# A two-layer diffusion trunk on eight cores: whole-tensor stages replaced by block streams that a list scheduler interleaves, with host-side layouts

## The chip, the cores and the metric

The kernel runs on all 8 cores of one Trainium2 chip; each core takes two of the 16 prompts and one of the 8 samples, and all share the weights. There is no traffic between cores. The metric is the time of the slowest core in device microseconds (us), as the median of several runs.

Runs come in two states. In the slow one the cores of a die show a lower granted TensorE clock (recorded in the trace as a share of full speed) and the time is longer: in the changed kernel's one slow run die 0 had 0.915 to 0.938 and die 1 0.945 to 0.964, and it took 1306.38 us where the median is 1277.59.

## The reference, cut to what matters

```
# 1536 tokens a core: two context sequences of 256, one latent sequence of 1024; D_MODEL = 1024
for i in range(DEPTH):                        # DEPTH = 2
    shift/scale/gate = ada_terms(cond, ada_w[i], ada_b[i])      # silu(cond) @ (1024 x 6144): "ada" below
    h = rms_norm(x, norm_mix_g[i]) * (1 + scale) + shift
    if i % 2 == 0:                            # pooling mixer beside latent attention
        u, cq, ckv, krope = ab_split(h, w_in)          # 512 + 384 + 256 + 32 columns
        y_pool = multi_scale_pool(u, pool_w, pool_scale)         # windows 2, 4, 8, 16
        q = rms_norm((rms_norm(cq) @ w_uq) per head)             # 8 heads of 64 + 32 rotary
        k = rms_norm(concat(ckv @ w_ukv, krope) per head); v = ckv @ w_ukv
        y = concat(y_pool, softmax(q k^T / sqrt(96)) v) @ w_out  # latent: 512 cached + 1024 own keys
    else:                                     # gated MLP over chunks of 128 tokens
        u, v = split(h @ gm_w_in); y = (u * (w_s rms_norm(v) + b_s)) @ gm_w_out
    x = x + gate * y
    x = x + gate2 * swiglu(rms_norm(x) modulated, wg, wu, wd)    # FFN, 2816 wide
```

The outputs are x for context and latent tokens, and the normalised `ckv` and the `krope` of the context.

## The kernel before

Every stage works on the whole tensor of 1536 tokens, and a stage begins when the one before it is through. x arrives token-major and is transposed on TensorE; its twelve tiles pass through a ring of four staging buffers.

```python
def load_transposed(src, ntile, F, dst3, ...):
    for i in range(ntile):
        P.dma("sp", st[:], src[i * 128:(i + 1) * 128, :], ...)
        ...
        P.tr(ps[...], st[:, fc * 128:fc * 128 + fp], ident[:])      # f32 transpose on TensorE
        P.cp(evac_engs[k % 2], dst3(f0, nb, i, fp), ps[...])

def xnorm(es2, l, w, hT, small=False):       # all three blocks, then the next stage
    for b in range(3):
        for kc in range(8):
            ... square on ScalarE or VectorE; P.mm(ps[:], ones[:], sq[:], ...)
        rstd(rs[:], ps[:], 1024)
        for kc in range(8): ... multiply, scale, shift
# ... [cut]
# attention: each head alone is projected, squared, normalised and rotated (72 such units)
def projq(ps, h=h, ...):
    P.mmg(ps[0:96, 0:n], [(wuq[:, kc, h * 96:(h + 1) * 96], cqn[:, kc, ...]) for kc in range(3)])
# ... [cut]
for hl in range(4):
    for (q0, n) in qblocks:
        for kt in range(nkt + 1):
            if kt < nkt:
                P.mm(S[:, 0:n], kT[0:96, hl, ...], qT[0:96, hl, q0:q0 + n])
                P.act(pt[:, 0:n], S[:, 0:n], AF.Exp, scale=float(96.0 ** -0.5))
            if pend is not None:
                P.mm(O[:, 0:n], Vsb[:, pk, hl, :], ppt[:, 0:n], ...)
        P.recip(rd[64:128, 0:n], O[64:128, 0:n])                     # softmax denominator, VectorE
        P.tt("dve", yab[0:64, ...], O[0:64, 0:n], rd[64:128, 0:n], ALU.mult)
        ada_piece(pool=(5, 6, 7))                                    # ring of three weight slots
```

Two helper lines recur in the profile: nearly all matmuls are recorded at L210, all ScalarE activations at L227.

## Time and profile before

| | before |
|---|---|
| fast runs | 1732 to 1744 us, median near 1740 |
| slow runs | one at 1793 us, the others 1866 to 1905 us |
| profiled run (fast, slowest core) | 1742.7 us |
| first input projection | 122 us |
| exps of attention, first to last | 346 to 710 us |
| first FFN matmul | 779 us |
| last matmul of the second FFN | 1702 us |

The prediction shows the busy shares and the stages. Three more lines carry the table: the answer for the exp tiles (count, duration in ns as least, median and most, first and last start), the row of the windows for the end (length, then busy us of PE, PEld, DVE, ACT, POOL, granted clock, DMA share, GB/s), and the count of DMA packets.

```profile
L227 ACT ACTIVATE pt<-pb x224: 378/597/597, 346.1 to 709.6; 128x512 bf16<-128x512 f32 x96, 128x256 bf16<-128x256 f32 x16
```
```profile
1702.00:1742.70 40.70, 14.72 (x98) 13.57 (x96) 8.98 (x14) 6.54 (x12) 0.00 (x0) 0.71 0.38 155
```
```profile
DMA packets 117684, 92.17 MB, mean 53 GB/s; under 512 B 4512, under 2 KB 104480, under 8 KB 117600
```

The exps are spread over 364 us, though 224 of at most 0.6 us need no more than 134. The last 41 us are output transposes and stores. Most packets are under 2 KB (104480 of 117684), because weight pieces are cut out of row-major matrices.

### The profile page before, as it was taken

The numbers are of one execution on the slowest core, as the hardware profiler recorded it, in microseconds if no ns is written. First come the engines' busy times: TensorE is split into PE (matmuls) and PEld (weight loads), VectorE is DVE, ScalarE is ACT, GpSimd is POOL, SyncE is SP. The second block draws the span as 40 slices with busy tenths as digits, with TensorE's granted clock in tenths as the row PEclk, the third lists the DMA queues.
The fourth block names the chain that finished last, engine by engine and source line by source line (L and its number), as shares of the span: only waits on it lengthen the run. The fifth ranks groups of instructions, "written<-read, shape, count | busy, mean of one in ns | idle before, by whom it ended". The sixth has DMA issues, their size and how long they took to land.

```text
span 1742.7 us, 17547 instructions; the slowest of 8 cores (1714.4 to 1742.7 us)
## 1 busy us (share of the span) xinstructions
PE 1320.0 (76%) x6107; PEld 573.0 (33%) x6211; DVE 677.6 (39%) x965; ACT 482.8 (28%) x884; POOL 320.9 (18%) x288
## 2 busy tenths in 40 slices
PE   3335661366877876959999999878847899999994
PEld 2202320133222221324444444323312344444443
DVE  1261224155444544462223243741825421424262
ACT  1141221244656656242110100143502311010101
POOL 1021106311620540032100000040421410000000
PEclk9757885555678669979999999979968899999997
DMA  9608642574040052007632313003060553340103
GB/s 193 121 0 97 87 52 73 81 97 61 1 61 13 0 90 32 0 0 104 89 49 40 46 25 49 1 6 49 1 97 0 85 82 52 54 55 2 24 1 145
DMA packets 117684, 92.17 MB, mean 53 GB/s; under 512 B 4512, under 2 KB 104480, under 8 KB 117600
## 3 DMA queue, kind: packets, MB, share of 16 engines
q0 software_dynamic: 110304, 72.10, 30.8%
q1 hardware_dynamic: 7296, 18.94, 3.2%
q8 instruction: 54, 0.88, 0.2%
q14 instruction: 30, 0.25, 0.1%
HBM read 156.24 MB, written 6.88 MB: 94 GB/s over the span
## 4 chain that ended last, share of the span: by engine, by line
PE 63%; DMA 11%; ACT 9%; DVE 8%; issue 5%; POOL 3%; ACTq 0%; SPq 0%; DVEq 0%; POOLq 0%
PE pb L210 60%; DMA adaw<-ada_w 5%; ACT pt L227 3%; PE pb L208 2%; ACT rsh L227 2%; DMA y<-ostg 2%; POOL hT L241 2%; DVE xtmp L231 1%; POOL S L231 1%; DMA ldt<-cckv 1%; DMA gwo<-gm_w_out 1%; ACT xrs L227 1%; DVE gtb L231 1%; ACT hT L227 1%; DMA ldt<-x_in 1%
## 5 line engine op out<-in xcount | busy, mean ns | idle before, releaser
L210 PE MATMUL pb<-hT,wgs 128*128 128x512 bf16 x1042 | 249.6, 380 | 1.0 <-POOL hT L241 0.2
L210 PE MATMUL pb<-hT,wus 128*128 128x512 bf16 x1029 | 247.1, 379 | 1.4
L248 DVE SCALAR_TENSOR_TENSOR xT<-pb,mod,xT 128x512 f32<-128x512 f32 x240 | 179.9, 751 | 149.0 <-PE pb L210 143.9
L210 PE MATMUL pb<-apart,wdb 128*128 128x512 bf16 x1035 | 227.6, 379 | 1.1
L231 DVE TENSOR_TENSOR apart<-pb,sg 128x512 bf16<-128x512 f32 x132 | 91.1, 691 | 352.8 <-PE pb L210 349.3
L227 ACT ACTIVATE sg<-pb 128x512 f32<-128x512 f32 x132 | 78.4, 597 | 484.3 <-PE pb L210 484.3
L210 PEld LDWEIGHTS pb<-hT,wgs 128*128 128x128 bf16 x1056 | 103.6, 98 | 126.4 <-issue 3.2
L210 PEld LDWEIGHTS pb<-apart,wdb 128*128 128x128 bf16 x1056 | 103.3, 98 | 124.6
L210 PEld LDWEIGHTS pb<-hT,wus 128*128 128x128 bf16 x1056 | 103.3, 98 | 124.4
L227 ACT ACTIVATE pt<-pb 128x512 bf16<-128x512 f32 (+1 forms) x224 | 117.9, 565 | 86.3 <-PE pb L210 84.6
L241 POOL TENSOR_SCALAR hT<-xtmp,AA,mod 128x512 bf16<-128x512 f32 x48 | 72.3, 1514 | 344.3 <-ACT hT L227 179.2
L260 DVE RECIPROCAL rd<-pb 64x256 f32<-64x256 f32 (+1 forms) x32 | 81.7, 2552 | 102.2 <-PE pb L210 102.1
L210 PE MATMUL pb<-pt,Vsb 128*128 128x512 bf16 (+1 forms) x214 | 84.9, 407 | 42.3 <-ACT pt L227 39.7
L210 PE MATMUL pb<-xsq,ones 128*128 128x512 bf16 x92 | 41.4, 545 | 84.1 <-ACT xsq L227 68.7
L210 PE MATMUL pb<-qT,kT 96*128 96x512 bf16 (+1 forms) x224 | 87.2, 414 | 10.4 <-DVE Vsb L254 4.7
L200 POOL DMA_DIRECT2D adaw<-ada_w x48 | 42.3, 883 | 237.9 <-PE pb L210 200.6
L231 DVE TENSOR_TENSOR xtmp<-xT,xrs 128x512 f32<-128x512 f32 x96 | 65.2, 727 | 37.8 <-ACT xrs L227 26.1
L227 ACT ACTIVATE xsq<-xT 128x512 bf16<-128x512 f32 x48 | 29.3, 624 | 179.5 <-PE pb L210 147.8
L210 PE MATMUL pb<-scT,adaw 128*128 128x2 bf16 x768 | 27.3, 165 | 57.5 <-DMA adaw<-ada_w 57.0
L210 PE MATMUL pb<-hT,w_in 128*128 128x512 bf16 (+1 forms) x230 | 68.9, 448 | 1.2 <-issue 0.8
L200 POOL DMA_DIRECT2D wgs<-ffn_wg x22 | 19.5, 888 | 262.8 <-PE pb L210 262.8
L210 PEld LDWEIGHTS pb<-pt,Vsb 128*128 128x128 bf16 x224 | 22.0, 98 | 138.1 <-issue 137.6
(119 smaller groups left out, 1384.2 us busy)
## 6 DMA issues: line engine op xcount, KB each, us to landing
adaw<-ada_w POOLq DMA_DIRECT2D x48, 512.0 KB, 9.5
wgs<-ffn_wg POOLq DMA_DIRECT2D x22, 512.0 KB, 5.8
wus<-ffn_wu POOLq DMA_DIRECT2D x22, 512.0 KB, 8.0
wdb<-ffn_wd POOLq DMA_DIRECT2D x22, 512.0 KB, 9.4
ldt<-x_in SPq DMA_DIRECT2D x12, 512.0 KB, 10.2
y<-ostg SPq DMA_DIRECT2D x12, 512.0 KB, 2.6
gws<-gm_w_in POOLq DMA_DIRECT2D x4, 1024.0 KB, 8.3
ic<-invcnt SPq DMA_DIRECT2D x4, 768.0 KB, 4.2
```

The source lines that it names most:

```text
L200: ins = eng.dma_start(out=out, in_=in_)
L208: return self.op("pe", lambda g: g.matmul(out, lhsT, rhs, start=start, stop=stop, skip_group_check=True), [lhsT, rhs], [out], inc=inc)
L210: return self.op("pe", lambda g: g.matmul(out, lhsT, rhs, start=start, stop=stop), [lhsT, rhs], [out], inc=inc)
L227: return self.op("act", lambda g: g.activation(out=out, in_=in_, func=func, bias=bias, scale=scale), reads, [out])
L231: return self.op(e, lambda g: g.tensor_tensor(out=out, in0=in0, in1=in1, op=op), [in0, in1], [out])
L241: return self.op(e, lambda g: g.tensor_scalar(out=out, in0=in0, scalar1=s1, scalar2=s2, op0=op0, op1=op1), reads, [out])
L248: return self.op(e, lambda g: g.scalar_tensor_tensor(out=out, in0=in0, scalar=sc, in1=in1, op0=op0, op1=op1), reads, [out])
L260: return self.op("dve", lambda g: g.reciprocal(out=out, in_=in_), [in_], [out])
```

## The change

The intent is to keep TensorE fed: what one block of 512 tokens waits for is to be filled with the matmuls of another block or another stage. A generator is written for each piece of work ("stream"), and a list scheduler with a time model of each engine decides, when the program is built, the order of instructions on every engine. The order is then fixed. Beside that: x, the caches, the weights and y are laid out on the host, so nothing is transposed on TensorE; the q heads are projected in groups of four, whose parts lie on different partitions and are brought into place by small copies through DMA; the key norm becomes a scale of the exp that is read from memory; the denominators are inverted by Ln and Exp on ScalarE; pooling, which VectorE and the pool engine shared before, goes to the pool engine alone. The diff, cut to its core:

```diff
+    def run(self, streams):
+        ...
+                t = self.est(u)                         # time model: when could this unit start
+                pe = "pe" in u.eng
+                slack = 30.0 if pe else 1500.0
+                key = (0, pe, s[0], t) if t <= now + slack else (1, t, s[0], 0)
 ...
+        issue = max(self.t[q], self._ready(evs, q))     # model of a DMA
+        self.t[q] = issue + (900.0 if q == "pool" else 60.0)
+        start = max(self.t[q], self.t_dma)
+        self.t_dma = start + n * esize(in_.dtype) / self.DMA_RATE
 ...
-            load_transposed(x_in, 12, 1024, lambda f0, nb, i, fp: xT[...], nring=4, per_tile=...)
+                for q in range(2):
+                    P.dma("sp", x[b][:, 4 * q:4 * q + 4, :], x_in[b][:, 4 * q:4 * q + 4, :], "x%d" % b)
 ...
-                P.dma("pool", sl[:], wview(ada_w[l])[:, :, c0 * 128:(c0 + 2) * 128], ...)
+                P.dma("pool", ada_ring[k][:], ada_d[k], "ada%d" % (k % 3))
 ...
-                                        P.mmg(ps[0:96, 0:n], [(wuq[:, kc, h * 96:(h + 1) * 96], ...
+                        P.mmg(ps[:], [(wq[:, kc, o:o + 128], cqn[b][:, kc, :]) for kc in range(3)])
+                        ...
+                        for j in range(4):
+                            P.dma("sp", qT[b][32 * c:32 * c + 32, hg * 4 + j, :], qh[32 * j:32 * j + 32, :],
+                                  "q%d_%d" % (b, hg))
 ...
-                                            P.act(pt[:, 0:n], S[:, 0:n], AF.Exp, scale=float(96.0 ** -0.5))
+                    P.act(pt[:, 0:n], S[:, 0:n], AF.Exp, scale=ksc[kb][:, kt, hd:hd + 1])
 ...
-                                        P.recip(rd[64:128, 0:n], O[64:128, 0:n])
+            P.act(rd[dn, :], O[dn, :], AF.Ln)
+            P.act(rd[dn, :], rd[dn, :], AF.Exp, scale=-1.0)
 ...
+        streams = [
+            (0, load_x("xi", (1, 2, 0))),
+            (1, ada_dma()),
+            (0, load_w0()),
+            (20, ada()),
+        ]                                               # number: rank, the lower goes first
+        ...
+            (6, win()), (10, kv()), (9, qproj()), (12, pool_grp()), (8, attention()), (1, load_wo()),
+        ...
+        streams += [(7, xnorm(0, 1, b, has("xm0_%d" % b), "h1_%d" % b)) for b in range(3)]
+        streams += [(2, ffn_load(0, ...)), (21, ffn(0, False))]
 ... [the rest of the rewrite cut]
```

## The prediction

> **What bounds the kernel now.** I read the list of runs first: 1737.6 and 1742.05 us are fast runs, 1888.83, 1901.5 and 1901.75 slow ones, so the stated median of 1888.83 is a slow run. The profiled run is fast (1742.7 us). I reason about the fast state and come to the slow one at the end. Then the page's busy shares and its 40 slices:
>
> ```profile
> PE 1320.0 (76%) x6107; PEld 573.0 (33%) x6211; DVE 677.6 (39%) x965; ACT 482.8 (28%) x884; POOL 320.9 (18%) x288
> ...
> PE   3335661366877876959999999878847899999994
> ...
> PEclk9757885555678669979999999979968899999997
> DMA  9608642574040052007632313003060553340103
> ```
>
> A slice is 43.6 us. TensorE is the only engine near saturation, but only in the right half. In the first 16 slices it is half busy and the granted clock is 0.5 to 0.8. The table of windows, cut at the stages that I read off the chain of waits, says which stage is which (columns: stretch, length, busy us with instruction counts for PE, PEld, DVE, ACT, POOL, then granted clock, DMA share, GB/s):
>
> ```profile
> 0.00:80.00 80.00, 29.38 (x236) 23.68 (x237) 11.80 (x35) 10.30 (x19) 8.82 (x14) 0.90 0.94 171
> 80.00:140.00 60.00, 15.36 (x31) 3.50 (x31) 32.73 (x37) 22.23 (x32) 12.60 (x15) 0.53 0.11 10
> 140.00:262.00 122.00, 80.04 (x537) 35.57 (x547) 25.04 (x52) 26.06 (x48) 13.87 (x16) 0.84 0.65 79
> 262.00:345.00 83.00, 16.68 (x47) 6.22 (x48) 23.47 (x25) 16.90 (x37) 42.82 (x27) 0.52 0.39 81
> 345.00:445.00 100.00, 67.52 (x454) 32.54 (x454) 56.47 (x95) 43.78 (x118) 15.21 (x17) 0.51 0.55 69
> 445.00:710.00 265.00, 206.12 (x684) 58.63 (x693) 121.62 (x151) 167.36 (x299) 82.29 (x72) 0.78 0.22 32
> ...
> 790.00:1122.00 332.00, 330.39 (x1509) 150.41 (x1539) 115.36 (x160) 38.87 (x65) 23.98 (x30) 1.00 0.37 53
> 1122.00:1159.00 37.00, 16.51 (x48) 5.13 (x47) 25.36 (x40) 20.87 (x30) 20.77 (x13) 0.72 0.00 0
> ```
>
> Loading bounds the first row, the first norm the second, the input projection with waits for ada pieces the third, the pooling the fourth, then attention. The feed-forward (FFN) rows are bound by TensorE at clock 1.00. The norms between stages (1122 to 1159; also 752 to 790, 1333 to 1357) leave TensorE half idle. The chain of waits gives the dense pitch, and the timeline gives two ScalarE pitches and the ada wait:
>
> ```profile
> 790.03 10.74 PE pb L210 x49
> ```
> ```profile
> 501.17 1.08 ACT L227 ACTIVATE pt<-pb 128x512 bf16<-128x512 f32 x2 [0.35 <-ACT pt L227]
> ```
> ```profile
> 286.97 1.26 ACT L227 ACTIVATE yab<-pb,vecs 128x512 bf16<-128x512 f32 x2 [3.92 <-PE pb L210]
> ```
> ```profile
> 142.52 0.56 PE L210 MATMUL pb<-scT,adaw 128*128 128x2 bf16 x16 [16.93 <-DMA adaw<-ada_w]
> ```
>
> 10.74/49 = 0.219 us for a 512-wide matmul. A lone exp takes 0.597 us and two take 1.08, so its pitch is 0.49 us; with a scale read from memory, two take 1.26 against 0.69 for one, pitch 0.57. Sixteen ada matmuls take about 0.51 us.
>
> [...] In the first 80 us the trace moves 171 GB/s as landed; as most of that is f32 read and landed as bf16, I estimate 275 GB/s read. [...] the trace has 5 loads of 1283 ns mean.
>
> **The change part by part.** The kernel is rewritten. The arithmetic is nearly the same; the order and the layouts are new.
>
> *TensorE work.* Counting the new kernel's instruction order: 4825 matmuls 512 wide (3168 FFN, 576 gated MLP, 384 attention, 240 input projection, 192 output projection, 96 norm sums, the rest small) and 64 of 256, together 4857 x 0.219 = 1065 us. Add 768 ada matmuls (48 x 0.51 = 24), 96 of 128 columns (about 10) and 80 tiny ones (about 2): 1101 us. Before, the same count gives 4963 x 0.219 = 1088, ada 24, 212 fp32 transposes (29.4 us of busy in the first window for half of them, so some 50): 1162 us. The change removes only about 60 us of TensorE work (the transposes, which the host layout replaces, and the head-by-head 96-row projections). The kernel before has 1743 - 1162 = 581 us of idle or cold time; that is what the change is after.
>
> *Idle time.* One program order built by a list scheduler, with blocks of 512 tokens as independent streams, takes the place of whole-tensor stages. I go along the new order:
>
> 1. Start. x arrives in 6.3 MB; the first ada pieces are issued by the pool engine only behind its squares of x, and from the fourth each waits for a slot of a ring of three, so they stream after x. Until the first projection: x, eight ada pieces at 1.05 MB read, w_ukv, the cached latent and w_ina, 19 MB. First x at about 340 GB/s (the hardware queue's 18.94 MB in 3.2% of the span) to 22 us, then 12.7 MB at 275 to 320, 40 to 46 us. First projection at 66 us; before it was at 122, and properly at 142.
>
> 2. Mixers. From 66 us, input projection, q, the first keys and values: about 330 matmuls, 75 us, so the first exp comes at about 141. From there to the last exp, ScalarE does 192 exps with a memory scale (0.57, 109 us), 32 half exps (0.36, 11), 24 pairs of Ln and Exp for the denominators (1.1, 26), and some 45 copies, squares and norms (24): 170 us. TensorE has about 130 us there, as ada and the first output projection fill in. So ScalarE is the bound; with 8% lost in the in-order interleave, 185 us. The DVE reciprocals (16 of 3.36 and 16 of 1.75 us) are gone, the 72 head norms become 6 joint ones for q and 4 small ones for k, and pooling (83 us alone before) runs on the pool engine beside attention. Mixers end at 326; with small stalls from the copies that assemble q and k through DMA I put 345.
>
> 3. The rest. x for two blocks is reloaded only as attention frees memory: 2 MB, 8 us, partly covered. Then 3936 matmuls x 0.219 = 863, spatial and ada work 17: 880 us dense, 1233. At the end of the first FFN the next norm must wait for a whole block while VectorE still updates residuals (24 x 0.75 = 18 us for 21 us of TensorE): 8 us of bubble. Other norms lie under other blocks' matmuls; 5 us for all, with extra table loads.
>
> 4. Tail. The result is stored as it is, without transposes: 6 us instead of 41.
>
> Sum: 345 + 8 + 880 + 13 + 6 = 1252; I say 1255, a gain of 485 us or 28% on the fast state. Of this about 60 is removed work, 56 to 76 the start, 35 the tail, 80 the norm gaps, and the rest pooling and attention.
>
> **Rivals.** (a) The static order misjudges durations and TensorE stalls in the mixers: q and k now pass through over 100 small copies on one in-order queue, while ada weights fill the rings. [...]this trace (copies of 36 to 384 KB landing in 5 to 9 us under load) allow it; 40 to 70 us more, 1300 to 1325. Against: attention has twelve key tiles per unit and other streams as filler. (b) ScalarE pitch is the isolated 0.69 and not 0.57: 224 x 0.12 = 27 us more. (c) VectorE or the pool engine becomes the bound: the pool engine carries all pooling, about 70 us before contention, plus 35 us of DMA issues, within 185; VectorE about 110. Both have slack. (d) Start bound at 340 GB/s and mixers hidden perfectly: 1200. [...] Slow minus fast before is 1897 - 1740 = 157 us[...]. This is a state and not a cost of the change, but it may set the median.
>
> **Range and chances.** The point is for fast runs. Fast outcomes lie between 1200 (d) and 1325 (a); three of five runs before were slow, and the median may be slow again[...]. I take 1200 to 1475 to hold both. Even a slow run here beats a fast one of before, so faster is nearly certain.
>
> **What would show it right or wrong.** In the new profile: first w_ina matmul at 60 to 75 us; first exp near 140; ScalarE over 85% busy from there to about 330; the FFN at 0.219 us a matmul and clock near 1.00; TensorE busy in every slice from the third on, with one dip between FFN and gated MLP; idle of TensorE in all about 150 us; fewer than 20 table loads. It would be wrong if the waits of TensorE name the q or k copies, or ada pieces, for over 30 us in sum, if the granted clock in the fast profile falls well under 1, or if the start lasts over 90 us.

Fast runs reach to 1325, by rival (a), and the 1475 stood for slow runs, by an estimate. Of the read rates of the start, 340 GB/s and 275 are worked out from the trace; 320 lies between them, and the prediction does not say where it comes from; at 275 alone the start would be 68 us.

## The result, and the profile after

The changed kernel ran 9 times: median 1277.59 us (1275.94 to 1306.38; one slow run). The kernel before, over 15 runs, had a median of 1741.17 us. The ratio of the fast runs is 0.735 with a 95% interval of 0.7336 to 0.7363. Every ratio in this document is the mean time of one kernel's fast runs over the mean time of the other's in the same rounds, so it is not quite the ratio of the medians.

The page of the changed kernel, profiled in a fast run (slowest core 1276.2 us; a slice is 31.9 us), answers to the same lines of before:

```profile
PE 1143.4 (90%) x5833; PEld 510.2 (40%) x5833; DVE 521.8 (41%) x862; ACT 416.7 (33%) x722; POOL 213.5 (17%) x258
...
PE   3179647887889999999999998999999999999998
...
PEclk9999768886899999999999998999999999999999
DMA  9970231479946688252085050003242332231005
...
DMA packets 33627, 103.31 MB, mean 81 GB/s; under 512 B 4688, under 2 KB 10448, under 8 KB 30992
```

From slice 13 on TensorE is full and the clock's digit is 9 (1.00 in the last of the windows below), with one 8 in either row between the first FFN and the gated MLP. What is left lies in slices 1 to 3 and 5 to 12: the load, and a stretch in which TensorE is at 0.4 to 0.8 and its clock dips to 0.6. The windows, cut at the new stages (columns as before):

```profile
0.00:68.00 68.00, 16.03 (x152) 6.93 (x152) 27.41 (x51) 12.88 (x19) 22.25 (x36) 1.00 0.99 210
...
153.00:210.00 57.00, 31.96 (x146) 12.12 (x144) 16.61 (x26) 25.27 (x47) 28.37 (x19) 0.70 0.29 64
210.00:270.00 60.00, 48.93 (x286) 19.45 (x286) 19.43 (x35) 48.28 (x82) 24.04 (x24) 0.86 0.46 89
270.00:345.00 75.00, 60.81 (x393) 24.49 (x394) 14.87 (x31) 68.81 (x126) 25.79 (x37) 0.77 0.91 163
345.00:396.00 51.00, 45.66 (x254) 18.72 (x253) 20.45 (x34) 40.17 (x68) 6.07 (x9) 0.90 0.49 82
...
765.00:800.00 35.00, 29.89 (x125) 12.65 (x124) 31.08 (x44) 15.42 (x27) 17.08 (x15) 0.90 0.00 1
...
950.00:1273.00 323.00, 322.85 (x1496) 146.18 (x1494) 120.85 (x169) 42.62 (x69) 10.62 (x20) 1.00 0.24 50
```

The load is bound by DMA (share 0.99). In the last row 322.85 us for 1496 matmuls is 0.2158 us each. Between 153 and 210 us neither engine is near its bound: ScalarE works 25 of 57 us, TensorE 32 with the clock at 0.70. The exps (columns as for before):

```profile
L360 ACT ACTIVATE pt<-pb,ksc x224: 455/689/770, 152.8 to 394.7; 128x512 bf16<-128x512 f32 x96, 128x256 bf16<-128x256 f32 x16
```

They now take 242 us instead of 364, and the first FFN matmul starts at 395.8 us, 1 us after the last exp, where before it was 70 us after it. The timeline of TensorE shows where the first stretch goes (start, length, instructions; in brackets the idle time before them and what ended it), and those of ScalarE and of SyncE's queue show why:

```profile
151.53 1.01 PE L347 MATMUL pb<-qT,kT 96*128 96x512 bf16 x2 [7.09 <-DMA kT<-kp]
166.67 1.01 PE L347 MATMUL pb<-ckvn,w_ukv 128*128 128x512 bf16 x2 [9.59 <-ACT rsr L360]
186.90 0.59 PE L347 MATMUL pb<-qT,kT 96*128 96x512 bf16 x1 [6.44 <-ACT ksc L360]
```
```profile
165.84 0.69 ACT L360 ACTIVATE rsr<-pb,epsc 128x512 f32<-128x512 f32 x1 [11.22 <-DMA qT<-qh]
```
```profile
161.56 11.31 SPq L303 DMA_DIRECT2D qT<-qh  x12
...
199.59 29.67 SPq L303 DMA_DIRECT2D qT<-qh  x28
```

TensorE names ScalarE at 166.67, but ScalarE itself had waited 11.22 us for a copy of q to land: a wait is to be followed to its end, and this one has two more steps. First, the instruction that waited reads only `pb` and `epsc`, not q. What it waited for was memory: its output lies where a tile had been out of which q is copied. Built again, kernel.py gives this tile the first 8 copies of its group of 12 as a condition, but the helper for waits raises this to every copy that has been put on the same semaphore, so it waited for the last 4 as well. The same holds for the two `sqr` tiles, whose waits for copies of k ended at 151.21 and 185.00: each needed 2 copies and waited for 8. From 143 to 215 us ScalarE waited 32 us for copies in this way. Second, those last 4 copies were late, because the queue stood 11.1 us for the pool engine to rotate q, and that engine had stood, in order, for the window counts of the pooling:

```profile
154.14 2.34 POOL L364 TENSOR_TENSOR pSb<-pSb,pic 128x1024 f32<-128x1024 f32 x1 [24.36 <-DMA pic<-invcnt]
```

The load of these counts was issued at 149.85 us on the same queue, behind two stores and 17 copies of q and k. No run here changes the placement of tiles or the semaphores. The queue issues 12 copies in 11.31 us, with waits inside; elsewhere in this trace eight q copies without a gap take 4.90 us and six k copies 3.91 us, 0.61 and 0.65 us each. The scheduler's model has 0.06. For the loads that the pool engine issues it has 0.9, where the weight loads here take 0.53 to 0.62 us each on the mean (an ada piece 0.555; in the kernel before, where the pieces are cut out of row-major matrices, 0.883). The whole table of TensorE's waits begins:

```profile
PE pb L347 <- DMA adaw<-ada_w: 24.9, 9, 3.7
PE pb L347 <- DVE xsq L364: 20.3, 8, 13.6
...
PE pb L347 <- DMA kT<-kp: 12.1, 2, 7.1
```

Of the 24.9 us for ada pieces, 19.3 lie in the first 68 us, in the start that loading bounds:

```profile
PE pb L347 <- DMA adaw<-ada_w: 19.3, 7, 3.7
```

Stage by stage, from the two profiled runs:

| | before | after | gained |
|---|---|---|---|
| start to the first input projection | 122.4 | 68.1 | 54 |
| from there to the last exp | 587.2 | 326.6 | 261 |
| from there to the first FFN matmul | 69.7 | 1.1 | 69 |
| from there to the last matmul (both FFNs, gated MLP, norms) | 923 | 877 | 46 |
| tail | 40.7 | 3.4 | 37 |
| sum | 1743 | 1276 | 467 |

The stages overlap in the changed kernel: 128 of the 192 matmuls of the output projection (28 us) come after the last exp and lie among those of the FFN, where before all 192 lay ahead of the FFN. So some 28 of the 69 us in the third row are moved into the fourth and not saved.

### The profile page after: what moved, and what is told of

Same layout as the page of the kernel before. It is cut to its first block, busy times and chain, and to the rows that moved or that the text cites. A ratio compares the mean times of both kernels' runs of the same rounds, so it can differ in the third digit from the quotient of the medians.

```text
span 1276.2 us, 16221 instructions; the slowest of 8 cores (1266.6 to 1276.2 us)
## 1 busy us (share of the span) xinstructions
PE 1143.4 (90%) x5833; PEld 510.2 (40%) x5833; DVE 521.8 (41%) x862; ACT 416.7 (33%) x722; POOL 213.5 (17%) x258
## 4 chain that ended last, share of the span: by engine, by line
PE 77%; DMA 8%; DVE 4%; ACT 4%; SPq 3%; issue 2%; POOL 1%; POOLq 0%; DVEq 0%; ACTq 0%
PE pb L347 77%; DMA adaw<-ada_w 3%; SPq L303 3%; DMA x<-x_in 2%; ACT pt L360 1%; DVE xtm L375 1%; ACT rd L360 1%; DMA w_ina<-w_ina 1%; DMA pic<-invcnt 1%; DVE x L375 1%; DVE h L370 1%; DMA kT<-kp 1%; DMA qT<-qh 0%; ACT rsr L360 0%; POOL pSb L364 0%
## 5 line engine op out<-in xcount | busy, mean ns | idle before, releaser
L347 PE MATMUL pb<-h,wg 128*128 128x512 bf16 x1056 | 250.3, 380 | 0.1
L347 PE MATMUL pb<-h,wu 128*128 128x512 bf16 x1056 | 249.5, 379 | 0.0
L364 DVE TENSOR_TENSOR a<-pb,sg 128x512 bf16<-128x512 f32 x132 | 91.2, 692 | 352.2 <-PE pb L347 341.2
L375 DVE SCALAR_TENSOR_TENSOR x<-pb,mod,x 128x512 f32<-128x512 f32 x240 | 179.1, 750 | 137.0 <-PE pb L347 127.6
L347 PE MATMUL pb<-a,wd 128*128 128x512 bf16 x1056 | 230.0, 379 | 0.0
L347 PEld LDWEIGHTS pb<-h,wu 128*128 128x128 bf16 x1056 | 103.3, 98 | 124.6
L347 PEld LDWEIGHTS pb<-a,wd 128*128 128x128 bf16 x1056 | 103.3, 98 | 124.0
L347 PEld LDWEIGHTS pb<-h,wg 128*128 128x128 bf16 x1056 | 102.6, 98 | 122.7 <-issue 1.9
L360 ACT ACTIVATE pt<-pb,ksc 128x512 bf16<-128x512 f32 (+1 forms) x224 | 133.0, 659 | 30.0 <-PE pb L347 28.8
L347 PE MATMUL pb<-qT,kT 96*128 96x512 bf16 (+1 forms) x224 | 97.2, 435 | 20.2 <-DMA kT<-kp 12.1
L347 PE MATMUL pb<-pt,V 128*128 128x512 bf16 (+1 forms) x224 | 95.6, 427 | 17.7 <-ACT pt L360 17.2
L347 PE MATMUL pb<-scT,adaw 128*128 128x2 bf16 x768 | 26.2, 165 | 25.1 <-DMA adaw<-ada_w 24.9
```

Source lines behind the costliest of these rows:

```text
L347: return self.op("pe", lambda g: g.matmul(out, lhsT, rhs, start=start, stop=stop, **kw), [lhsT, rhs], [out], (c, 190), inc=inc)
L360: return self.op("act", lambda g: g.activation(out=out, in_=in_, func=func, bias=bias, scale=scale, **kw), reads, writes, d)
L364: return self.op(e, lambda g: g.tensor_tensor(out=out, in0=in0, in1=in1, op=op), [in0, in1], [out], self._d(e, out, [in0, in1], "tt"))
L375: return self.op(e, lambda g: g.scalar_tensor_tensor(out=out, in0=in0, scalar=sc, in1=in1, op0=op0, op1=op1), reads, [out], self._d(e, out ...
```

## The experiments

Two questions were open: what cost the 50 us by which the mixers ended later than predicted, and what made up the gain. All kernels here were reported correct. The ratios are to the fast runs of the kernel before; the changed kernel stands at 0.735. The kernels went to the chip in groups, so two of them are best compared by their ratios.

### The queue's issue time put into the scheduler's model

```diff
-        self.t[q] = issue + (900.0 if q == "pool" else 60.0)
+        self.t[q] = issue + (560.0 if q == "pool" else 640.0)
```

No instruction changes, only the order that the scheduler makes of them.

> The scheduler's own cost of a DMA issue is set to what the trace shows: 0.64 us on the SyncE queue (it assumed 0.06) and 0.56 us on the pool engine (it assumed 0.9). Nothing else changes. Queue theory (the mixers' missing time is lost because 108 small copies of q and k share one in-order queue and the static order believed them free): 20 to 35 us less, about 1242 to 1257, with TensorE's waits on k copies and on the engines behind them between 140 and 210 us mostly gone. ScalarE theory (the mixers are bound by ScalarE whatever the order): within 6 us of 1277. Both: the stretch from the end of the mixers on stays at 877 us.

Measured: 1261.71 us, ratio 0.7268 [0.7252, 0.7284], 16 us less than the changed kernel. The same stretches as above:

```profile
153.00:210.00 57.00, 33.51 (x152) 12.58 (x154) 15.94 (x25) 28.48 (x53) 29.60 (x20) 0.73 0.27 62
210.00:270.00 60.00, 50.48 (x328) 19.75 (x334) 18.36 (x36) 57.42 (x101) 26.09 (x27) 1.00 0.52 94
```

From 210 us on the theory holds: ScalarE works 57 of 60 us instead of 48, TensorE's clock is 1.00 instead of 0.86, and the last exp starts at 380 instead of 395. Between 153 and 210 next to nothing changed: the pool engine still stands 24.1 us for the window counts, and ScalarE 10.6 us for a copy of q, by the same line of code and so again for memory. So the corrected model explains some 15 of the 50 us, less than expected. Two numbers were changed at once, and any new number makes a new order; no run tells what SyncE's number did alone.

### In addition, the k copies on another queue

```diff
-                        P.dma("sp", kT[kb][0:64, 2 * p + o, :], kp[64 * o:64 * o + 64, :], "kp%d" % kb)
+                        P.dma("pool", kT[kb][0:64, 2 * p + o, :], kp[64 * o:64 * o + 64, :], "kp%d" % kb)
```

(And the same for the copy of the rotary keys; on top of the run above.)

> As e1, and the 36 copies that assemble k are issued from the pool engine's queue, so that SyncE keeps the 72 of q. Queue theory: 5 to 15 us less again than e1 (1230 to 1250), first exp before 148 us. Rival: the pool engine issues in order behind pooling and ada loads, so the k copies come late there, and it is no faster than e1 or up to 15 us slower.

Measured: 1263.44 us, ratio 0.7276 [0.7261, 0.7291], no better than without. The first exp came at 148.2 instead of 152.0, the last at 365.8 instead of 380.1. Between 153 and 210 us both engines now work more:

```profile
153.00:210.00 57.00, 42.71 (x274) 18.00 (x273) 20.26 (x38) 34.91 (x64) 32.79 (x35) 0.77 0.52 108
```

So part of that loss could be removed: the last exp is 29 us earlier than in the changed kernel. But the table of waits for 270 to 430 us begins

```profile
PE pb L347 <- DMA adaw<-ada_w: 13.4, 1, 13.4
```

The gain of 14 us in the mixers turned into one wait for an ada weight piece. The ada multiplications rank behind everything but the FFNs and the gated MLP, so they are used as filler; as soon as attention is faster, they come before their weights.

### A constant scale in the exp

```diff
-                    P.act(pt[:, 0:n], S[:, 0:n], AF.Exp, scale=ksc[kb][:, kt, hd:hd + 1])
+                    P.act(pt[:, 0:n], S[:, 0:n], AF.Exp, scale=0.1)
```

Wrong: the keys are then not normalised. The comparison with the reference did not flag it, so its verdict of correct is no proof that this part of the arithmetic is right.

> Wrong result on purpose: the exps take a constant scale instead of one read from memory per key. Everything else is as in the changed kernel. The exp pitch should go from 0.58-0.59 to 0.49 us, 224 x 0.09 = 20 us of ScalarE. ScalarE theory: 15 to 20 us less in total. Queue theory: only the part after 250 us, where ScalarE is over 90% busy, gains, about 8 to 12 us less.

Measured: 1272.61 us (1266.43 to 1280.33), ratio 0.7332 [0.7278, 0.7386]; the interval holds the changed kernel's 0.735. The exps did get shorter, 597 ns against 689:

```profile
L360 ACT ACTIVATE pt<-pb 128x512 bf16<-128x512 f32 x192 | 104.4, 597 | 34.9 <-PE pb L347 33.9
```

Twelve in a row take 6.32 us in this trace and 7.08 us with the scale from memory, a pitch of 0.527 against 0.590. For 192 exps that would be 12 us if ScalarE were the bound throughout; 5 us by the medians came out. The four runs lie in two pairs, near 1266 and near 1279, and the interval reaches from some 13 us faster to 6 slower. So the price of the folded key norm is at most some 13 us, and this run cannot tell for how much of the mixers ScalarE was the bound.

### VectorE's reciprocal back in the denominators

```diff
-            P.act(rd[dn, :], O[dn, :], AF.Ln)
-            P.act(rd[dn, :], rd[dn, :], AF.Exp, scale=-1.0)
+            P.op("dve", lambda g: g.reciprocal(out=rd[dn, :], in_=O[dn, :]), [O[dn, :]], [rd[dn, :]], (3300.0, 80))
```

> The softmax denominators go back to one VectorE reciprocal each (3.36 us for 512 columns in the kernel before), in place of Ln and Exp on ScalarE. This undoes that part alone. ScalarE theory: it frees 48 passes of 0.55 to 0.6 us, 26 to 29 us, and the time falls by 10 to 25 us. Rival (the long reciprocals block the in-order VectorE, and the accumulator bank is held 3 us longer): the time rises by 5 to 20 us. VectorE has about 70 us of work in the 243 us of attention, so 24 x 3.36 = 81 us fit.

Measured: 1268.59 us, ratio 0.7306 [0.7289, 0.7323], 9 us less. In the changed kernel, replacing the reciprocal is a loss. The row of the reciprocals (busy us, mean ns of one, idle time before them):

```profile
L886 DVE RECIPROCAL rd<-pb 64x512 f32<-64x512 f32 x24 | 80.4, 3350 | 13.7 <-PE pb L347 13.4
```

80 us on VectorE, which has room (111 of 328 us in the mixers of the changed kernel), against 29 us of Ln and Exp on ScalarE, which works 221 of these 328 us. The last exp came 20 us earlier (374.6), and 10.5 us of waits for ada pieces followed: again half of it given back.

### The same exchange in the kernel before

```diff
-                                        P.recip(rd[64:128, 0:n], O[64:128, 0:n])
+                                        P.act(rd[64:128, 0:n], O[64:128, 0:n], AF.Ln)
+                                        P.act(rd[64:128, 0:n], rd[64:128, 0:n], AF.Exp, scale=-1.0)
```

> The kernel before with one part of the change alone: Ln and Exp on ScalarE in place of the VectorE reciprocals (82 us of VectorE busy). If the reciprocals were on its path, up to 30 us less. My view: in the 512-wide units they lie under the next unit's exps, and the two added ScalarE passes (1.1 us x 32) cost there what the 256-wide units gain: within 15 us of the kernel before, ratio 0.99 to 1.01.

Measured: 1755.59 us, ratio 1.0085 [1.0047, 1.0122], 15 us slower. So this part of the change costs time in both kernels.

### The layouts alone, in the kernel before

First x, the caches and y (no transposes), then the weights too:

```diff
-            load_transposed(x_in, 12, 1024, lambda f0, nb, i, fp: xT[:, f0:f0 + nb, i * 128:(i + 1) * 128], nring=4, ...)
+            for b in range(3):
+                for q in range(2):
+                    P.dma("sp", xT[:, 4 * q:4 * q + 4, b * 512:(b + 1) * 512], x_in[b][:, 4 * q:4 * q + 4, :], "x%d" % b)
 ... and for the second run
-                P.dma("pool", sl[:], wview(ada_w[l])[:, :, c0 * 128:(c0 + 2) * 128], "adaw%d" % (k % 3))
+                P.dma("pool", sl[:], ada_w[k], "adaw%d" % (k % 3))
 ... and likewise for every weight
```

> The kernel before with another part alone: x, the cached latent and y are laid out by the host feature-major, so that 212 fp32 transposes, their copies and the staging are gone. Tail: 41 us becomes about 6, so 35 less. Start: bound by loading, but the cached latent's eight small serial loads (50 to 80 us in the trace) go, 15 to 30 less. Together 50 to 65 us less, ratio 0.962 to 0.972. If the transposes' TensorE time counted in full (50 us) on top, it would be over 90 less.

> The kernel before with everything that the changed kernel lays out on the host: x, the caches and y as in the run before host layout (which gave 53 us), and now every weight piece contiguous for each partition as well, so that the descriptors become fewer and larger (the changed kernel has 33627 packets where the one before has 117684). No reordering. Loading theory: the waits of TensorE for ada pieces and w_in come partly from small packets; 20 to 40 us less than the 1686 us of the x, cache and y layout alone, so 1645 to 1665. Rival: the loads are bound by bytes read, and the ada pieces by the ring of three and the pool engine's turn; then no more than 10 us, 1676 to 1690. Either way the layouts would be 55 to 95 of the 464 us, and the order has the rest.

Measured: 1686.38 us, ratio 0.9681 [0.964, 0.9721], for the first; 1675.32 us, ratio 0.9632 [0.9598, 0.9667], for both. The first came out as expected, 53 us. Contiguous weights are worth 11 us more by the medians and 8 by the ratios, whose intervals overlap; that is near the rival's 10, although the packets fell to a quarter:

```profile
DMA packets 28242, 91.85 MB, mean 55 GB/s; under 512 B 4000, under 2 KB 5056, under 8 KB 27136
```

So the number of packets was little of what bound the loads. All layouts together are 64 of the 464 us between the medians; the order and the regrouped work have the rest.

### Barriers put back at the three later norms

```diff
-        streams += [(7, xnorm(0, 1, b, has("xm0_%d" % b), "h1_%d" % b)) for b in range(3)]
+        streams += [(7, xnorm(0, 1, b, has("xm0_0", "xm0_1", "xm0_2"), "h1_%d" % b)) for b in range(3)]
 ... and likewise for the two norms of layer 1
```

> The changed kernel with one part undone: each norm between stages (after the output projection, after the first FFN, after the gated MLP) waits until all three blocks of tokens are through the stage before, as in the kernel before. The sum of the prediction put 80 us on these gaps; if that is their worth, 1340 to 1365. Rival: since a norm still streams block by block into the next stage, only the first block's norm is exposed, about 15 us at each of three places, and the rest of the 80 us came with the streaming: 1310 to 1330.

Measured: 1358.09 us, ratio 0.78 [0.7771, 0.7829]: 80 us, exactly what the prediction had for the norm gaps. It would have been easy to stop there. But the table of waits begins

```profile
PE pb L347 <- DMA adaw<-ada_w: 69.6, 21, 5.8
```

against 24.9 us in the changed kernel (19 us of either lie in the start): 45 of the 80 us appear as waits for ada pieces, which the scheduler used up around the barriers, before their weights had come.

### The same barriers, with the ada pieces out of the way

The next kernel joins what the earlier runs pointed to (issue times, k copies on the pool queue, reciprocal) and multiplies ada pieces as they land:

```diff
-            (20, ada()),
+            (5, ada()),
```

> The changed kernel with what the earlier runs pointed to, together: issue times of 640 ns on the copy queue and 560 ns on the pool engine in the scheduler's model, the k copies on the pool engine's queue, the VectorE reciprocal in place of Ln and Exp in the softmax denominators, and ada pieces multiplied as soon as they land (rank 5 in place of 20), so that their loads run on beside attention. Theory: the mixers end near 355 to 365 (366 to 375 with each alone), and the ada waits of 10 to 13 us that took half of it back in those runs go, as the DMA share of 0.3 to 0.5 between 153 and 270 us has room for the loads: 1235 to 1250. Rival: the loads are bound by the ring of three, and TensorE, now made to wait for each piece in its order, stalls on them in the mixers: 1260 or more.

Measured: 1269.94 us, ratio 0.7304 [0.7281, 0.7327]: the rival's number, but not its mechanism, for after the first 68 us TensorE waits for no ada piece at all. Taken alone, the model's numbers and the reciprocal gave 16 and 9 us; together they give 8. The last exp did come early, at 371.8 us, 8 us before the first run's 380.1. But the output projection now lies wholly behind it:

```profile
L347 PE MATMUL pb<-ya,wo x93: 379/379/379, 373.8 to 418.9; 128*128 128x512 bf16 x93
```

In the first run it lay beside the end of attention (334.2 to 400.8), so that the first FFN matmul came at 402.4 us, and here at 419.1. That is where the gain went. Inside attention one chain of lines shows a further stall (SyncE's queue, the pool engine, TensorE):

```profile
260.32 18.96 SPq L303 DMA_DIRECT2D qT<-qh  x24
```
```profile
282.91 0.72 POOL L364 TENSOR_TENSOR pSb<-pSb,pic 128x256 f32<-128x256 f32 x1 [14.44 <-DMA pic<-invcnt]
```
```profile
292.91 0.37 PE L347 MATMUL pb<-qT,kT 96*128 96x256 bf16 x1 [14.97 <-DMA kT<-kp]
```

The load of the pooling's window counts sits in SyncE's queue behind 24 copies of q until 279 us. The pool engine waits 14.4 us for it, in order, and behind it wait a fill of V and the k copies that now also go through that engine. TensorE stands for 15 us. Moving the k copies to another queue made that queue's other work part of attention's path.

On this kernel the barriers were tried again:

> The kernel of the run all three (1270 us, ratio 0.7304) with the barriers of the run norm barriers: each of the three later norms waits for all three blocks of x. In the run norm barriers the cost was 80 us, but 45 of them were TensorE waits on ada pieces, as pieces that serve as filler were used up around the barrier; here the pieces are multiplied as they land, long before. Theory: a norm gap by itself costs some 10 to 15 us of idle or half-clock TensorE at each of three boundaries, 30 to 45 us in all: 1300 to 1315. Rival, the predicted 80 us for the norm gaps: 1345 to 1355.

Measured: 1309.14 us, ratio 0.7529 [0.7504, 0.7553], 39 us more than without barriers. So on this kernel, in which no ada wait interferes (none between 396 and 1000 us), the norm gaps are worth about 39 us, half of what the prediction had. (The half clock of the expectation is seen in such a gap of the kernel before: 0.50 from 760 to 780 us.)

### Barriers put back inside the mixers

```diff
-                yield U("dve", cond=has("cache_loaded" if kb == 3 else "kv%d" % kb), ...)
+                yield U("dve", cond=has("cache_loaded" if kb == 3 else "kv%d" % kb, "u_ctx"), ...)
 ... q likewise; attention waits for all k, q and the pooling; the output projection for the end of attention
```

> The changed kernel with another part undone: keys, values and q start when the whole input projection is done, attention when all of them and the pooling are done, the output projection when attention is done. If the overlap inside the mixers is what made them short (rival to the queue theory), the end of attention moves from 387-395 us to 420-450 and the total rises by 30 to 60 us. Queue theory: the early attention was stalled on copies anyway (ScalarE busy 25 of 57 us between 153 and 210), so hardly anything is lost: within 15 us of 1277.

Measured: 1368.06 us, ratio 0.7857 [0.7827, 0.7887], 90 us more, and more than either theory had. Attention alone then runs well, from 307.9 to 475.8 us, at the end with ScalarE saturated:

```profile
410.00:470.00 60.00, 51.37 (x175) 12.19 (x173) 5.28 (x8) 59.46 (x103) 0.17 (x1) 0.97 0.25 62
```

The price is paid before it: 62 us of TensorE work in the 142 us from 128 on, with the chains of norms, copies and pooling laid bare. As in the first barrier run, part of it is ada: waits of 62 us against 25. So 90 us is an upper figure for the overlap in the mixers, not a clean one.

### A shorter start

On the first run's kernel: only block 1 of x is loaded at first, the squares of the first norm stay off the pool engine, `w_ina` follows the eight ada pieces at once, and the other blocks of x come later on the same queue.

```diff
-            (0, load_x("xi", (1, 2, 0))),
+            (0, load_x("xi", (1,))),
 ... in load_w0, after w_ina:
+            yield from load_x("xi", (2,), "pool")
 ... after w_inu:
+            yield from load_x("xi", (0,), "pool")
```

> The run queue in model (1261.7 us, ratio 0.7268) with a shorter start: only block 1 of x is loaded first, the first norm keeps its squares off the pool engine, so that the eight ada pieces are issued at once, w_ina follows straight behind them, and the blocks 2 and 0 of x, w_ukv and the cached latent come later on the same queue. 13.2 MB are then read before the first projection in place of 19. Theory: loading bounds the start, so the first w_ina matmul comes at 48 to 56 us in place of 68, the granted clock and the waits after it permitting 8 to 15 us of the end: 1246 to 1254. Rival: the later stage until the first exp is bound by the bytes that still have to come (w_inu, w_uq, the other blocks of x) and by the chain of norms, so that the first exp stays at 150 us and the time at 1260.

Measured: 1300.58 us, ratio 0.7479 [0.7457, 0.7501], 39 us slower than its base, which neither theory had. The start itself did what was asked: the first input projection at 50.8 us instead of 68, the first exp at 123.3 instead of 152.0, the last at 372.8 instead of 380.1. But the first FFN matmul came at 457.0 instead of 402.4. The output projection's matmuls (first and last start), in the base and in this kernel:

```profile
L347 PE MATMUL pb<-ya,wo x96: 379/379/631, 334.2 to 400.8; 128*128 128x512 bf16 x96
```
```profile
L347 PE MATMUL pb<-ya,wo x96: 379/379/634, 404.8 to 455.9; 128*128 128x512 bf16 x96
```

In the base it lay beside the end of attention, here after it, and 24 us of waits for ada pieces lie between the two. The scheduler made a new order for everything behind the start: the first exp came 29 us earlier, the first FFN matmul 55 us later. A better order behind the early start may exist; no run here shows one.

No combination beat the first run: 1261.7 us, two changed numbers in the scheduler's model, is the best version measured, 1.2% faster than the changed kernel (16 of 1277.6).

## Why the prediction was right or wrong, point by point

The sum was 1252 us and the profiled run has 1276; the deviations are +50, -24 and -3.

**Start.** 68.1 against 66 us, bound by loading (DMA share 0.99). Right.

**The mixers.** Predicted to end at 345, they ended at 394.7. This is the step that failed: "ScalarE is the bound; with 8% lost in the in-order interleave", and "small stalls from the copies". Of the 50 us, 12 are the late first exp (152.8 against 141; 2 of them from the start), 12 more work on ScalarE than the 170 us summed, and 26 more idle time: ScalarE was busy 183 of 243 us, so that 60 were lost, 25% and not 8%, where the prediction had allowed 34 (15 for the interleave, 19 for the copies). ScalarE is near its bound only between 270 and 345 us (69 of 75). Rival (a) named the place: q and k copies on one in-order queue, in a static order with a wrong time for them. The condition set down for being wrong (waits on copies or ada pieces over 30 us in sum) was met with 12.1 + 24.9 = 37 us, but only by counting the start; from 68 us on it is 12.1 + 5.7 = 18. What the copies cost shows on ScalarE, which waited 32 us for them between 143 and 215 us, for memory tied to them and not for q or k. A copy of q by itself landed in 1.9 us at the median, and not in the 5 to 9 us of rival (a).

The experiments share out the 50 us only in part. The last exp came 15 us earlier with the corrected model, 29 with the k copies on another queue as well, 20 with the reciprocal (which takes 29 us of work off ScalarE), and 23 with all of these. So they do not add up, and part of what was won came back later each time. Two rivals have no run. One is the memory and the semaphores shared by the copies. The other is the clock: TensorE was given 130 us of work there, and was busy 187 us at a granted clock of 0.80; at the dense pitch its matmuls would take about 140 us (my estimate: 552 of 512 columns at 0.2158 us, 64 of 256 at half of that, 25 sets of ada at 0.51 us). How much of the delay each of these makes stays open.

**The denominators.** The prediction counted the lost reciprocals as gain and their replacement as 26 us of ScalarE (29 in the trace). Two runs show that the exchange costs 9 us here and 15 us in the kernel before. Wrong in sign.

**The exp's pitch.** 0.57 us was taken from another instruction with a scale in memory; twelve exps in a row have 0.59, the end of the last one counted in. Right; rival (b) fell. For a constant scale the 0.49 drawn from two exps was too low; twelve have 0.527. So a scale from memory costs 92 ns in the median exp (689 against 597) and 63 ns a piece in a row.

**The rest.** 877 us against 901 (8 + 880 + 13). The dense pitch was mis-sized: 10.74/49 counts the last matmul with its whole 0.379 us (48 x 0.2158 + 0.379 = 10.74), and the pitch in the window of 323 us is 0.2158; for 3936 matmuls that is 13 us. The other 11 us are bubbles that came out smaller: from 396 to 1273 us TensorE is busy 867 of 877 us, so 10 us are idle where the prediction allowed 21 for the reload, the bubble and the norms.

**The tail.** 3.4 against 6 us. Right.

**The granted clock.** It was 1.00 in the dense stages; in the window of 323 us it was so on all eight cores, and no core of the profiled run has a mean under 0.942. The prediction's estimate of the slow state, which gave the 1475 us, failed: the one slow run in nine had 1306.38, 2.3% over the median, with die 0 at 0.915 to 0.938 against 0.942 to 0.962 in the profiled run. Other slow runs lost 7% (1452 in the group of the norm barriers) and 10% (1509 in that of the mixers). The slow state's size is not explained by anything here.

**Where the gain was put.** Start 54 (56 to 76 predicted) and tail 37 (35) hold, nearly. Norm gaps: 39 and not 80. The mixers are the bulk: 261 us up to the last exp and about 41 of the 69 after it. Up to 90 of these are overlap, by the barriers. With those barriers in, the changed kernel still needs only 409 us from the first projection to the last exp (67.1 to 475.8), where the kernel before needs 587. That this difference of 178 us belongs to regrouped work (joint q and k norms, pooling off TensorE's path, exps in one run) is argued from these traces, not shown by a run that undoes it.

**The signs set down.** Idle time of TensorE (133 us, about 150 foreseen) and table loads (15, fewer than 20) came as said. ScalarE over 85% busy in the mixers (75%) and TensorE busy in every slice from the third on (0.4 to 0.8 in slices 5 to 12) did not.

The close hit on the total, 1277.6 for 1255, is therefore partly luck, two errors that cancel: 50 us too little for the mixers, 24 too much for what follows.

## What to carry to other kernels

In a static order, give the queue's issue time for each DMA to the model like any engine's time: with two such numbers put right (0.64 us for SyncE and 0.56 for the pool engine here) the kernel became 16 us faster. Follow a wait on a copy to its end: here ScalarE stood for memory tied to copies under one semaphore for a whole group, and the copies stood behind another engine. When a stage gets faster, look at once at what it used as filler and at what loads feed that filler: in four of the runs here (k copies, reciprocal, all three, shorter start) half or more of a gain in attention came back as a wait for weights or as work pushed behind it. And when an experiment hits the predicted number exactly, read its waits before believing it: the 80 us of the norm barriers were some 39 of norms and the rest exposed loads.
